# Turning activations by VectorE over all partitions and a round trip through device memory, in a two-layer macaron encoder

## The chip, the cores and the metric

The kernel runs on one core of a Trainium2 chip. Its time is device microseconds of one launch; 920.27 us is the median of three runs of the kernel before (919.97 to 920.5). One further execution was profiled; all durations below come from it.

## What is computed

Two identical layers act on a 256 x 1024 float32 array `x` (256 positions), and a last RMSNorm follows:

```python
for l in range(DEPTH):
    x = x + 0.5 * swiglu(rms_norm(x, norm_ffn1[l]), ffn1_w_gate[l], ffn1_w_up[l], ffn1_w_down[l])
    h = rms_norm(x, norm_mix[l])
    q, k, v, u, g = jnp.split(h @ w_in[l], splits, axis=-1)
    a = dilated_attention(partial_rotary(heads(q)), partial_rotary(heads(k)), heads(v))
    sg = spatial_gating(u, g, ...)
    x = x + concat([rms_norm(a), rms_norm(sg)]) @ w_out[l]
    x = x + 0.5 * swiglu(rms_norm(x, norm_ffn2[l]), ffn2_w_gate[l], ffn2_w_up[l], ffn2_w_down[l])
return rms_norm(x, final_norm)
```

`swiglu(h)` is `(silu(h @ w_gate) * (h @ w_up)) @ w_down`; the hidden width is 2816. Every weight is float32 and is used once.

## The kernel before

**Products.** The 256 positions lie in two tiles of 128 partitions (`NT`). A float32 product is made of three matmuls on float32 operands that were split into a high part and a rest: high x high, high x rest, rest x high (L165 to L167). The left operand has to be turned, so that the contracted channel lies on the partitions: `xTh`, `xTl` for `x`, and `hT` (high and rest) for the hidden activations `h`.

**Units.** The weights come as a stream of 164 units of at most four blocks of 128 x 512 (`UNITS`, 1 MB each; some hold two blocks). `load_unit` issues a unit's DMA on SP's queue into one of three `raw` buffers. `split_unit` makes the high part `whi` on ACT (L133) and the rest `wlo` on VectorE (L134), each in two instructions of 128 x 1024, into one of three buffers of each kind. `multiply` uses the unit: 4 blocks x 2 tiles x 3 = 24 matmuls on PE. A buffer comes round every third unit, so **the split of a unit has to wait until PE is done with the unit three places ahead of it in the stream**, and a load until the split of the unit three places ahead is done.

**Order.** The engines run their instructions strictly in program order. The code states an order, and the tile framework's scheduler then places each instruction by its own estimate of when it becomes ready; so an instruction can end up some places away from where the code puts it. SP's queue is in order too: a DMA that waits holds up all those behind it.

**Stages.** `ffn` works through six chunks of 512 hidden channels (the last has 256) and then through `w_down` in two passes, one for each half of `x`'s columns; `add`s bring the result into `x_sb` (L461). `mixer` starts with the first halves (channels 0 to 511) of q, k and v, and then takes their second halves. In what follows **q0, k0, v0** are the units with the first halves and **q1, k1, v1** those with the second; **a0 to a5** are the six units of the first pass through the `w_down` ahead of it, **b0 to b5** those of the second pass. a5 and b5 hold two blocks instead of four. PE takes them in the order a0 ... a5, b0 ... b5, q0, k0, v0, q1, k1, v1.

**Turning.** Where there is time, VectorE turns: its transpose swaps rows and columns within blocks of 32 x 32. `turn_blocks` (L271 to L276) uses it with 32 partitions in and another 32 partitions out, so that each block also lands in the right group of 32 partitions (a quadrant): 16 instructions of 32 x 256 for a chunk. `h_turn` and `turn_slowly` call it in four parts of four, spread between the products, and finish with the split into high part and rest (L279, L280 for `h`; L322, L323 for `x`). The first half of `x` at the start of each second ffn goes another way, through PE (`turn`). `turned` has one buffer, `h` two.

The half of `x` that is turned last is needed when PE gets to the second halves: in the mixer after three units (q0, k0, v0), at the start of an ffn after four.

Of the kernel before, what the change touches and what calls it, by code (L numbers as in the profile page):

```python
# [10 lines left out]
F32 = mybir.dt.float32  # L11
F32R = mybir.dt.float32r
BF16 = mybir.dt.bfloat16
AF = mybir.ActivationFunctionType
ALU = mybir.AluOpType
PSUM = bass.MemoryType.PSUM

P = 128
D = 1024
S = 256  # L20
NT = S // P
# [9 lines left out]
W = 512  # L31
NCH = FF // W
REM = FF - NCH * W
# [54 lines left out]
def trunk_kernel(ctx: ExitStack, tc: tile.TileContext, ws, x, cxt, rows, sgw, ident, bias, rot, out):  # L88
    nc = tc.nc
# [3 lines left out]
    big = ctx.enter_context(tc.tile_pool(name="big", bufs=1))  # L93
    act = ctx.enter_context(tc.tile_pool(name="act", bufs=4))
    small = ctx.enter_context(tc.tile_pool(name="small", bufs=4))
    ps_acc = ctx.enter_context(tc.tile_pool(name="ps_acc", bufs=4, space=PSUM))
    ps_sc = ctx.enter_context(tc.tile_pool(name="ps_sc", bufs=4, space=PSUM))

    def f32(ap):
        return ap.bitcast(F32)  # L100
# [102 lines left out]
    def accumulators(name, pool=None, tag="acc"):  # L203
        return [(pool or ps_acc).tile([P, W], F32, tag=tag, name=f"{name}{t}") for t in range(NT)]
# [8 lines left out]
    x_sb = const.tile([P, NT, D], F32, name="x_sb")  # L213
# [37 lines left out]
    def col(l, c):  # L251
        return cols_sb[:, l * NCOL + c:l * NCOL + c + 1]
# [15 lines left out]
        nc.gpsimd.tensor_tensor(v[:, 2], v[:, 1], half.to_broadcast([P, NT]), op=ALU.pow)  # L268
        return v[:, 2]

    def turn_blocks(dst, src, c):  # L271

        to = dst.rearrange("p k (t b j) -> p t k b j", t=NT, b=4)
        frm = src.rearrange("p t (k c i) -> p t k c i", c=4, i=32)
        for b in range(4):
            nc.vector.transpose(to[32 * c:32 * c + 32, :, :, b, :], frm[32 * b:32 * b + 32, :, :, c, :])  # L276

    def split_turned(dst_hi, dst_lo, src):
        nc.scalar.activation(dst_hi, src, AF.Copy)  # L279
        nc.vector.tensor_tensor(dst_lo, src, f32(dst_hi), op=ALU.subtract)  # L280
# [15 lines left out]
    class Stream:  # L296
# [16 lines left out]
        def turn_slowly(self, d, part):  # L313

            if part == 0:
                self.turned = act.tile([P, 4, S], F32, tag="turned", name="turned", bufs=1)
            turn_blocks(self.turned, x_sb[:, :, d * W:(d + 1) * W], part)
            if part == 3:
                for k in range(4):
                    g = col(self.l, self.c + 4 * d + k)  # L320
                    hi, lo = self.lhs(4 * d + k)
                    nc.scalar.activation(hi, self.turned[:, k], AF.Copy, scale=g)  # L322
                    nc.vector.scalar_tensor_tensor(lo, self.turned[:, k], g, f32(hi), op0=ALU.mult, op1=ALU.subtract)  # L323

        def given(self, k):

# [30 lines left out]
    def ffn(st, nxt, turn_second):  # L357

        hT = [[None, None] for _ in range(3)]
        turned = {}  # L360

        def h_group(f):
            a = f // 8
            if hT[a][0] is None:
                hT[a] = [big.tile([P, 8, S], F32R, tag=f"h{2 * a + n}", name=f"hT{n}") for n in range(2)]
            return hT[a]

        def h_lhs(f):
            hi, lo = h_group(f)
            return hi[:, f % 8], lo[:, f % 8]  # L370

        def h_turn(f0, h, part):

            n = h.shape[2] // P
            if part == 0:
                turned[f0] = act.tile([P, 4, S], F32, tag="turned", name="turned", bufs=1)
            turn_blocks(turned[f0][:, :n], h, part)
            if part == 3:
                for j in range(0, n, 2):
                    hi, lo = h_group(f0 + j)  # L380
                    a = (f0 + j) % 8
                    split_turned(hi[:, a:a + 2], lo[:, a:a + 2], turned[f0][:, j:j + 2])

        def gated(gate, w):
            ss = []
            for t in range(NT):
                s = act.tile([P, W], F32, tag="s", name="s")
                nc.scalar.activation(s[:, :w], gate[t], AF.Silu, scale=r[:, t:t + 1])
                ss.append(s)
            return ss  # L390

        def product(ss, up, w):
            h = act.tile([P, NT, W], F32, tag="h", name="h", bufs=2)
            for t in range(NT):
                nc.vector.scalar_tensor_tensor(h[:, t, :w], up[t], r[:, t:t + 1], ss[t][:, :w],
                                               op0=ALU.mult, op1=ALU.mult)
            return h[:, :, :w]


        accs = [accumulators("gate"), accumulators("up"),  # L400
                accumulators("gate", ps_sc, "sc"), accumulators("up", ps_sc, "sc")]
        if UNITS[done["used"]][1].endswith("_first"):
            multiply_first(accs, st.lhs)
            for i in range(len(accs)):
                turn_second(i)
        else:
            for i, acc in enumerate(accs):
                multiply(acc, st.lhs, True, False)
                turn_second(i)
        r = inverse_root(st.ssq, D)  # L410
        late = None
        for c in range(2):
            multiply(accs[2 * c], st.lhs, False, True)
            ss = gated(accs[2 * c], W)
            multiply(accs[2 * c + 1], st.lhs, False, True)
            h = product(ss, accs[2 * c + 1], W)
            if late:
                for q in range(4):
                    h_turn(*late, q)
            late = (c * W // P, h)  # L420
        for c in range(2, NCH):
            gate = accumulators("gate")
            multiply(gate, st.lhs, True, False)
            h_turn(*late, 0)
            multiply(gate, st.lhs, False, True)
            ss = gated(gate, W)
            h_turn(*late, 1)
            up = accumulators("up")
            multiply(up, st.lhs, True, False)
            h_turn(*late, 2)  # L430
            multiply(up, st.lhs, False, True)
            h_turn(*late, 3)
            late = (c * W // P, product(ss, up, W))
        both = accumulators("both")
        multiply(both, st.lhs, True, False)
        h_turn(*late, 0)
        h_turn(*late, 1)
        multiply(both, st.lhs, False, True)
        ss = gated([b[:, :REM] for b in both], REM)
        h_turn(*late, 2)  # L440
        h_turn(*late, 3)
        late = (NCH * W // P, product(ss, [b[:, REM:] for b in both], REM))
        new = None
        for d in (0, 1):
            acc = accumulators("down")
            if d == 1 and isinstance(new, Last):
                for k0 in range(0, 16, 4):
                    multiply(acc, h_lhs, k0 == 0, k0 == 12)
                new.begin(acc)
                for part in multiply_apart(h_lhs, 2):  # L450
                    new.finish(*part)
                break
            for k0 in range(0, KF, 4):
                multiply(acc, h_lhs, k0 == 0, k0 + 4 >= KF)
                if d == 0 and k0 <= 12:
                    h_turn(*late, k0 // 4)
                if d == 1 and k0 <= 12:
                    new.turn_slowly(0, k0 // 4)
            for t in range(NT):
                xs = x_sb[:, t, d * W:(d + 1) * W]  # L460
                nc.vector.scalar_tensor_tensor(xs, acc[t], 0.5, xs, op0=ALU.mult, op1=ALU.add)  # L461
            if d == 0:
                new = nxt()
            new.squares(d)
        return new
# [45 lines left out]
    def mixer(l, st, nxt):  # L511

        accs = [accumulators("q"), accumulators("k"), accumulators("v", ps_sc, "sc")]
        for i, acc in enumerate(accs):
            multiply(acc, st.lhs, True, False)
            for part in ((0, 1), (2, 3), ())[i]:
                st.turn_slowly(1, part)
        r = inverse_root(st.ssq, D)
        r8 = small.tile([P, NT], F32, tag="r8", name="r8")
# [226 lines left out]

def _stream(inputs):
    parts = []  # L750
    for l, name, ks, c in UNITS:
        if name.endswith("_first"):
            tiles = [inputs[name[:4] + m][l][c * P:(c + 1) * P, cc * W:(cc + 1) * W]
                     for cc in range(2) for m in ("_w_gate", "_w_up")]
            parts.append(np.concatenate(tiles, axis=1).reshape(-1))
            continue
        if name.endswith("_rem"):
            f = name[:4]
            w = np.concatenate([inputs[f"{f}_w_gate"][l][:, NCH * W:], inputs[f"{f}_w_up"][l][:, NCH * W:]], axis=1)
        else:  # L760
            w = inputs[name][l]
        k0, n = ks[0], len(ks)
        block = w[k0 * P:(k0 + n) * P, c * W:(c + 1) * W].reshape(n, P, W).transpose(1, 0, 2)
        parts.append(np.ascontiguousarray(block).reshape(-1))
    return np.concatenate(parts)
# [53 lines left out]
```

## Time and profile before

| | |
|---|---|
| median of three runs | 920.27 us (919.97 to 920.5) |
| the profiled execution | 922.07 us |
| its span, first to last instruction | 920.3 us |
| ScalarE (ACT) busy | 466.3 us |
| GpSimd (POOL) busy | 21.5 us |
| moved by DMA | 174.14 MB |

The span is what the profile's rows fill; 1.77 us of the profiled execution lie around it. In a group of instructions the name left of the arrow is what is written, the names right of it what is read; a line number (L276) is that of the kernel before, and lines of the changed kernel are told as such.

### The profile page before, as it was taken

To read this page: it belongs to the slowest core of one execution; us is meant where nothing else is said; L and a number is where in the kernel's file an instruction comes from. 1 tells how busy PE (TensorE), PEld (TensorE's weight loads), DVE (VectorE), ACT (ScalarE), POOL (GpSimd) and SP (SyncE) were. 2 spreads that over 40 slices of the span, in tenths; PEclk is the share of its full clock that TensorE was granted. 3 is DMA by queue.
4 is the path that set the end of the run, shared out by engine and by line. 5 is a ranking of instruction groups with operands and counts; after the bars stand their busy time and mean duration, and the time that the engine had idled before them with its cause. 6 is when DMAs were issued, how large, how long until landed. Compare 5 with 4: busy or idle time off the path is not lost.

```text
span 920.3 us, 11062 instructions
## 1 busy us (share of the span) xinstructions
PE 912.4 (99%) x4178; PEld 750.2 (82%) x4178; DVE 751.1 (82%) x1203; ACT 466.3 (51%) x654; POOL 21.5 (2%) x48
## 2 busy tenths in 40 slices
PE   9999999999999999999999999999999999999997
PEld 6888888888778888888888888888887888888886
DVE  6698996796789699896687998966887887998854
ACT  6544544356756544434445544445467545444440
POOL 0000000000010000000000000000000100000000
PEclk9999999999999999999999999999999999999999
DMA  8765555565334645646555555455543455565351
GB/s 330 297 259 183 187 201 205 187 217 192 138 113 175 215 141 206 219 147 237 192 197 177 192 213 191 152 209 208 201 140 135 164 202 183 183 210 200 126 195 47
DMA packets 26982, 174.14 MB, mean 189 GB/s; under 512 B 3120, under 2 KB 4272, under 8 KB 6960
## 3 DMA queue, kind: packets, MB, share of 16 engines
q1 hardware_dynamic: 26496, 172.86, 52.6%
q8 instruction: 33, 0.54, 0.2%
q10 hardware_dynamic: 432, 0.56, 0.2%
q14 instruction: 21, 0.17, 0.1%
HBM read 172.36 MB, written 1.05 MB: 188 GB/s over the span
## 4 chain that ended last, share of the span: by engine, by line
PE 97%; DVE 1%; issue 1%; ACT 0%; DMA 0%; POOL 0%; POOLq 0%; DVEq 0%
PE down L165 8%; PE down L166 8%; PE down L167 8%; PE gate L166 7%; PE up L166 7%; PE up L167 7%; PE gate L167 7%; PE up L165 7%; PE gate L165 7%; PE both L166 2%; PE both L165 2%; PE both L167 2%; PE g L165 1%; PE q L167 1%; PE g L166 1%; PE os L165 1%
## 5 line engine op out<-in xcount | busy, mean ns | idle before, releaser
L134 DVE TENSOR_TENSOR wlo<-raw,whi 128x1024 fp32r<-128x1024 f32 (+2 forms) x325 | 378.4, 1201 | 105.1 <-ACT whi L133 102.8
L133 ACT ACTIVATE whi<-raw 128x1024 fp32r<-128x1024 f32 (+2 forms) x325 | 322.4, 1039 | 246.9 <-issue 100.1
L276 DVE STREAM_TRANSPOSE turned<-h 32x256 f32<-32x256 f32 (+1 forms) x384 | 158.9, 414 | 6.3
L167 PE MATMUL down<-whi,hT 128*128 128x512 f32 x340 | 132.3, 389 | 0.0
L165 PE MATMUL down<-whi,hT 128*128 128x512 f32 x340 | 132.3, 389 | 0.0
L166 PE MATMUL down<-wlo,hT 128*128 128x512 f32 x340 | 132.3, 389 | 0.0
L167 PE MATMUL gate<-whi,xTl 128*128 128x512 f32 x304 | 118.3, 389 | 0.0
L167 PE MATMUL up<-whi,xTl 128*128 128x512 f32 x304 | 118.3, 389 | 0.0
L166 PE MATMUL gate<-wlo,xTh 128*128 128x512 f32 x304 | 118.3, 389 | 0.0
L165 PE MATMUL up<-whi,xTh 128*128 128x512 f32 x304 | 118.3, 389 | 0.0
L166 PE MATMUL up<-wlo,xTh 128*128 128x512 f32 x304 | 118.3, 389 | 0.0
L165 PE MATMUL gate<-whi,xTh 128*128 128x512 f32 x304 | 118.1, 389 | 0.0
L167 PEld LDWEIGHTS down<-whi,hT 128*128 128x128 f32 x340 | 63.8, 188 | 13.3
L165 PEld LDWEIGHTS down<-whi,hT 128*128 128x128 f32 x340 | 63.8, 188 | 13.3
L166 PEld LDWEIGHTS down<-wlo,hT 128*128 128x128 f32 x340 | 63.8, 188 | 13.2
L279 ACT ACTIVATE hT<-turned 128x512 fp32r<-128x512 f32 x44 | 26.8, 626 | 80.2 <-DVE turned L276 80.2
L165 PEld LDWEIGHTS gate<-whi,xTh 128*128 128x128 f32 x304 | 57.1, 188 | 11.9
L165 PEld LDWEIGHTS up<-whi,xTh 128*128 128x128 f32 x304 | 57.1, 188 | 11.9
L166 PEld LDWEIGHTS up<-wlo,xTh 128*128 128x128 f32 x304 | 57.1, 188 | 11.9
L166 PEld LDWEIGHTS gate<-wlo,xTh 128*128 128x128 f32 x304 | 57.1, 188 | 11.9
L167 PEld LDWEIGHTS up<-whi,xTl 128*128 128x128 f32 x304 | 57.1, 188 | 11.8
L167 PEld LDWEIGHTS gate<-whi,xTl 128*128 128x128 f32 x304 | 57.0, 188 | 11.8
(172 smaller groups left out, 1064.7 us busy)
## 6 DMA issues: line engine op xcount, KB each, us to landing
raw<-in_ws SPq DMA_DIRECT2D x154, 1024.0 KB, 4.8
raw<-in_ws SPq DMA_DIRECT2D x8, 512.0 KB, 3.2
raw<-in_ws SPq DMA_DIRECT2D x7, 256.0 KB, 5.5
x_sb<-in_x SPq DMA_DIRECT2D x1, 1024.0 KB, 10.8
ln_sb<-in_rows SPq DMA_DIRECT2D x1, 1024.0 KB, 7.4
out<-y SPq DMA_DIRECT2D x2, 320.0 KB, 2.5
xt_sb<-in_cxt SPq DMA_DIRECT2D x1, 512.0 KB, 7.9
sgw_sb<-in_sgw SPq DMA_DIRECT2D x1, 512.0 KB, 6.5
```

The lines of the kernel that those rows point to most:

```text
L133: nc.scalar.activation(hi[:, s], raw[:, s], AF.Copy)
L134: nc.vector.tensor_tensor(lo[:, s], raw[:, s], f32(hi[:, s]), op=ALU.subtract)
L165: nc.tensor.matmul(acc[t], xh[:, s], wh, start=start and j == 0, stop=False)
L166: nc.tensor.matmul(acc[t], xh[:, s], wl, start=False, stop=False)
L167: nc.tensor.matmul(acc[t], xl[:, s], wh, start=False, stop=stop and j == len(ks) - 1)
L276: nc.vector.transpose(to[32 * c:32 * c + 32, :, :, b, :], frm[32 * b:32 * b + 32, :, :, c, :])
L279: nc.scalar.activation(dst_hi, src, AF.Copy)
```

## The change

A turn is made in two steps. VectorE transposes the 32 x 32 blocks in place in their quadrant, over all 128 partitions at once: one instruction of 128 x 512 for each of the two tiles. Then `move_quadrants` stores the result in device memory (`far`) and loads it back with four DMAs, one for each quadrant of the destination, in rows of 512 bytes. So a turn has 2 transposes instead of 16, and 5 DMAs on SP's queue. Of the four parts of a turn only the first (transposes and moves) and the last (the split) are left. The hidden channels come out in another order within a chunk, and the rows of `w_down` are put into that order ahead of the launch (`F_ORDER`). The splits read `turned` in runs of 32 elements.

```diff
+    far = ctx.enter_context(tc.tile_pool(name="far", bufs=3, space=bass.MemoryType.DRAM))
...
-    def turn_blocks(dst, src, c):
-
-        to = dst.rearrange("p k (t b j) -> p t k b j", t=NT, b=4)
-        frm = src.rearrange("p t (k c i) -> p t k c i", c=4, i=32)
-        for b in range(4):
-            nc.vector.transpose(to[32 * c:32 * c + 32, :, :, b, :], frm[32 * b:32 * b + 32, :, :, c, :])
+    def move_quadrants(dst, tmp):
+
+        n = dst.shape[2]
+        store = far.tile([NT * P, 4 * n], F32, tag="far", name="far")
+        nc.sync.dma_start(store.rearrange("(t p) f -> p t f", p=P), tmp)
+        for c in range(4):
+            nc.sync.dma_start(dst[32 * c:32 * c + 32],
+                              store[:, c * n:(c + 1) * n].rearrange("(q i) f -> i q f", i=32))
...
         def turn_slowly(self, d, part):
             if part == 0:
-                self.turned = act.tile([P, 4, S], F32, tag="turned", name="turned", bufs=1)
-            turn_blocks(self.turned, x_sb[:, :, d * W:(d + 1) * W], part)
+                tmp = act.tile([P, NT, W], F32, tag="h", name="xB", bufs=2)
+                for t in range(NT):
+                    nc.vector.transpose(tmp[:, t].rearrange("p (c k j) -> p k c j", c=4, j=32),
+                                        x_sb[:, t, d * W:(d + 1) * W].rearrange("p (k c i) -> p k c i", c=4, i=32))
+                self.turned = act.tile([P, 4 * NT, W // 4], F32, tag="turned", name="turned", bufs=1)
+                move_quadrants(self.turned, tmp)
...
             if part == 0:
-                turned[f0] = act.tile([P, 4, S], F32, tag="turned", name="turned", bufs=1)
-            turn_blocks(turned[f0][:, :n], h, part)
+                for t in range(NT):
+                    nc.vector.transpose(h[:, t], h[:, t])
+                turned[f0] = act.tile([P, 4 * NT, W // 4], F32, tag="turned", name="turned", bufs=1)[:, :, :32 * n]
+                move_quadrants(turned[f0], h)
...
         for i, acc in enumerate(accs):
             multiply(acc, st.lhs, True, False)
-            for part in ((0, 1), (2, 3), ())[i]:
+            for part in ((0,), (), (3,))[i]:
                 st.turn_slowly(1, part)
```

The last lines are those of the mixer: the first part stands behind q0 as before, the split, which stood behind k0, now stands behind v0.

**Place 1: the start of the first mixer.** ACT's program there, in the kernel before; `whi` rows are splits (two instructions to a unit), `junk` the square sums, `xTh` the split of the turned second half of `x`, `qk<-q` the first use of what q1 finishes:

```order
L257 ACTIVATE junk,ssq<-x_sb 128x512 x2
L133 ACTIVATE whi<-raw 128x1024 x4
L322 ACTIVATE xTh<-turned,cols_sb 128x256 x4
L133 ACTIVATE whi<-raw 128x1024 x2
L526 ACTIVATE qk<-q_1482,r_1613 128x512
```

The same place of ACT's program in the changed kernel:

```order
L258 ACTIVATE junk,ssq<-x_sb 128x512
L134 ACTIVATE whi<-raw 128x1024 x2
L258 ACTIVATE junk,ssq<-x_sb 128x512
L134 ACTIVATE whi<-raw 128x1024 x6
L337 ACTIVATE xTh<-turned,cols_sb 128x256 x4
L540 ACTIVATE qk<-q_1429,r_1553 128x512
```

The last unit split ahead of `qk` is v1 in both. Before, `xTh` stands between the splits of k1 and v1; now the splits of q1, k1 and v1 all stand ahead of it.

VectorE's program at the same place, before (`x_sb<-down` are the additions at the end of the second pass, `xTl` the rest of the split of `x`, `ab` belongs to what follows q1):

```order
L461 SCALAR_TENSOR_TENSOR x_sb<-down_1271,x_sb 128x512
L461 SCALAR_TENSOR_TENSOR x_sb<-down_1272,x_sb 128x512
L134 TENSOR_TENSOR wlo<-raw,whi 128x1024 x2
L276 STREAM_TRANSPOSE turned<-x_sb 32x2x4x32 x8
L134 TENSOR_TENSOR wlo<-raw,whi 128x1024 x2
L276 STREAM_TRANSPOSE turned<-x_sb 32x2x4x32 x8
L134 TENSOR_TENSOR wlo<-raw,whi 128x1024 x2
L323 SCALAR_TENSOR_TENSOR xTl<-turned,cols_sb,xTh 128x256 x4
L134 TENSOR_TENSOR wlo<-raw,whi 128x1024 x2
L533 TENSOR_TENSOR ab<-qk,rot_sb 128x128
```

And in the changed kernel:

```order
L475 SCALAR_TENSOR_TENSOR x_sb<-down_1225,x_sb 128x512
L135 TENSOR_TENSOR wlo<-raw,whi 128x1024 x2
L475 SCALAR_TENSOR_TENSOR x_sb<-down_1226,x_sb 128x512
L135 TENSOR_TENSOR wlo<-raw,whi 128x1024 x2
L328 STREAM_TRANSPOSE xB<-x_sb 128x4x4x32 x2
L135 TENSOR_TENSOR wlo<-raw,whi 128x1024 x6
L338 SCALAR_TENSOR_TENSOR xTl<-turned,cols_sb,xTh 128x256 x4
L547 TENSOR_TENSOR ab<-qk,rot_sb 128x128
```

The same swap: `wlo` of v1 stood behind `xTl` and now stands ahead of it. k0's `wlo` has moved from ahead of the additions to between them. The second layer's mixer has v1 ahead of `xTh` and `xTl` in the same way.

SP's queue of the changed kernel at this place:

```order
L120 DMA raw<-in_ws 128x2048 x5
L276 DMA far<-xB 128x2x512
L120 DMA raw<-in_ws 128x2048
L278 DMA turned<-far 32x8x128 x4
```

The store, a load of one unit of weights, and then the four loads that bring the data back. Before, only the `raw` rows stood here.

**Place 2: the end of the first pass through the first `w_down`.** VectorE's program before, from the splits up to the first transposes:

```order
L461 SCALAR_TENSOR_TENSOR x_sb<-down_1063,x_sb 128x512
L461 SCALAR_TENSOR_TENSOR x_sb<-down_1064,x_sb 128x512
L134 TENSOR_TENSOR wlo<-raw,whi 128x1024 x2
L276 STREAM_TRANSPOSE turned<-x_sb 32x2x4x32 x7
L134 TENSOR_TENSOR wlo<-raw,whi 128x1024 x2
```

And in the changed kernel:

```order
L290 TENSOR_TENSOR hT_1017<-turned,hT_1016 128x512
L475 SCALAR_TENSOR_TENSOR x_sb<-down_1025,x_sb 128x512
L475 SCALAR_TENSOR_TENSOR x_sb<-down_1026,x_sb 128x512
L328 STREAM_TRANSPOSE xB<-x_sb 128x4x4x32
L135 TENSOR_TENSOR wlo<-raw,whi 128x1024 x2
L328 STREAM_TRANSPOSE xB<-x_sb 128x4x4x32
```

Here the `wlo` behind the additions was that of b2; it is now that of b1, with a transpose ahead of it. On PE the matmuls of a5 (12 of them, into the accumulators of the first pass, `down0_1025` and `down1_1026`) have moved behind the first 16 of b0's 24. The changed kernel's rows where they begin, with the tiles' numbers (`whi_1166` is b0's, `whi_1134` a5's):

```order
L168 MATMUL down0_1225<-whi_1166,hT1_507 128x512
L166 MATMUL down1_1226<-whi_1166,hT0_506 128x512
L166 MATMUL down0_1025<-whi_1134,hT0_1016 128x512
L167 MATMUL down0_1025<-wlo_1135,hT0_1016 128x512
L166 MATMUL down1_1026<-whi_1134,hT0_1016 128x512
L168 MATMUL down0_1025<-whi_1134,hT1_1017 128x512
```

Apart from this place and the order of two matmuls in b1, PE's program is the same as before. In the other three ffns a5 stays ahead of b0.

**Place 3: the start of an ffn.** ACT's program at the start of the first layer's second ffn, before and then in the changed kernel:

```order
L133 ACTIVATE whi<-raw 128x1024 x5
L322 ACTIVATE xTh<-turned,cols_sb 128x256 x4
L133 ACTIVATE whi<-raw 128x1024 x4
L388 ACT_TABLE_LOAD
L388 ACTIVATE s<-gate_2327,root 128x512
```

```order
L134 ACTIVATE whi<-raw 128x1024 x7
L337 ACTIVATE xTh<-turned,cols_sb 128x256 x4
L134 ACTIVATE whi<-raw 128x1024 x2
L405 ACT_TABLE_LOAD
L405 ACTIVATE s<-gate_2267,root 128x512
```

`xTh` has moved behind one more split. Here four units precede the first use of the second half, and the last split ahead of `xTh` is that of the sixth unit, which takes the buffer of the third.

More of the change, by code (lines that the diff above doesn't have):

```diff
@@ L269, in inverse_root, with turned_tile, as_blocks @@
         return v[:, 2]
-    def turn_blocks(dst, src, c):
-        to = dst.rearrange("p k (t b j) -> p t k b j", t=NT, b=4)
-        frm = src.rearrange("p t (k c i) -> p t k c i", c=4, i=32)
-        for b in range(4):
-            nc.vector.transpose(to[32 * c:32 * c + 32, :, :, b, :], frm[32 * b:32 * b + 32, :, :, c, :])
+    def move_quadrants(dst, tmp):
[5 more added lines that the diff above has]
+                              store[:, c * n:(c + 1) * n].rearrange("(q i) f -> i q f", i=32))
+    def turned_tile(turned, k, n):
+        return turned.rearrange("p q (k j) -> p k q j", j=32)[:, k:k + n]
+    def as_blocks(ap):
+        return ap.rearrange("p k (q j) -> p k q j", j=32)
     def split_turned(dst_hi, dst_lo, src):
@@ L320, in turn_slowly @@
                     g = col(self.l, self.c + 4 * d + k)
-                    hi, lo = self.lhs(4 * d + k)
-                    nc.scalar.activation(hi, self.turned[:, k], AF.Copy, scale=g)
-                    nc.vector.scalar_tensor_tensor(lo, self.turned[:, k], g, f32(hi), op0=ALU.mult, op1=ALU.subtract)
+                    hi, lo = (v[:, 4 * d + k].rearrange("p (q j) -> p q j", j=32) for v in (self.hi, self.lo))
+                    src = turned_tile(self.turned, k, 1)[:, 0]
+                    nc.scalar.activation(hi, src, AF.Copy, scale=g)
+                    nc.vector.scalar_tensor_tensor(lo, src, g, f32(hi), op0=ALU.mult, op1=ALU.subtract)
         def given(self, k):
@@ L381, in h_turn @@
                     a = (f0 + j) % 8
-                    split_turned(hi[:, a:a + 2], lo[:, a:a + 2], turned[f0][:, j:j + 2])
+                    split_turned(as_blocks(hi[:, a:a + 2]), as_blocks(lo[:, a:a + 2]), turned_tile(turned[f0], j, 2))
         def gated(gate, w):
@@ L415, in ffn @@
             multiply(accs[2 * c + 1], st.lhs, False, True)
+            if late:
+                h_turn(*late, 0)
             h = product(ss, accs[2 * c + 1], W)
[L417 to L420, printed above, removed]
+            first, late = late, (c * W // P, h)
         for c in range(2, NCH):
@@ L423, in ffn @@
             multiply(gate, st.lhs, True, False)
+            if c == 2:
+                h_turn(*first, 3)
             h_turn(*late, 0)
@@ L426, in ffn @@
             ss = gated(gate, W)
-            h_turn(*late, 1)
             up = accumulators("up")
             multiply(up, st.lhs, True, False)
-            h_turn(*late, 2)
             multiply(up, st.lhs, False, True)
@@ L436, in ffn @@
         h_turn(*late, 0)
-        h_turn(*late, 1)
         multiply(both, st.lhs, False, True)
         ss = gated([b[:, :REM] for b in both], REM)
-        h_turn(*late, 2)
         h_turn(*late, 3)
@@ L745, in trunk_kernel, with _tile_order @@
         st = ffn(st, Last if l == DEPTH - 1 else (lambda: Stream(l + 1, 0)), turn)
+def _tile_order(n, tiles):
+    return np.arange(n).reshape(-1, 4, tiles, 32).transpose(0, 2, 1, 3).reshape(-1)
+F_ORDER = np.concatenate([_tile_order(NCH * W, W // P), NCH * W + _tile_order(REM, REM // P)])
 def _stream(inputs):
@@ L761, in _stream @@
             w = inputs[name][l]
+            if name.endswith("_down"):
+                w = w[F_ORDER]
         k0, n = ks[0], len(ks)
```

## The prediction

> **What bounds the kernel now.** First the page: busy time by engine, the granted clock, and the chain of work that ended last.
>
> ```profile
> span 920.3 us, 11062 instructions
> PE 912.4 (99%) x4178; PEld 750.2 (82%) x4178; DVE 751.1 (82%) x1203; ACT 466.3 (51%) x654; POOL 21.5 (2%) x48
> PEclk9999999999999999999999999999999999999999
> PE 97%; DVE 1%; issue 1%; ACT 0%; DMA 0%; POOL 0%; POOLq 0%; DVEq 0%
> ```
>
> TensorE (PE) is busy in 912.4 of 920.3 us at full clock, and 97% of the chain is its matmuls. So time is lost or won only where PE waits. The table of waits tells where PE, or its weight load (PEld), waited once it was running:
>
> ```profile
> PEld q L167 <- DVE xTl L323: 0.5, 2, 0.2
> PE mixed L690 <- DVE vv L658: 0.2, 1, 0.2
> ```
>
> That is next to nothing: the most that a faster VectorE could give back is these 0.7 us. But the first row shows where there is no cover: at q's second half (q1) PE waits for the turned `x`, twice, once a layer. Now the timeline of that place in the first layer, first ACT, then VectorE (DVE), then PE (start, duration, what, how many):
>
> ```profile
> 187.32 2.01 ACT L133 ACTIVATE whi<-raw 128x1024 fp32r<-128x1024 f32 x2 [0.71 <-PE down L167]
> 192.81 2.01 ACT L133 ACTIVATE whi<-raw 128x1024 fp32r<-128x1024 f32 x2 [2.26 <-issue]
> 198.25 2.01 ACT L133 ACTIVATE whi<-raw 128x1024 fp32r<-128x1024 f32 x2 [3.43 <-issue]
> 201.06 1.71 ACT L322 ACTIVATE xTh<-turned,cols_sb 128x256 fp32r<-128x256 f32 x4 [0.80 <-DVE turned L276]
> 203.69 2.01 ACT L133 ACTIVATE whi<-raw 128x1024 fp32r<-128x1024 f32 x2 [0.92 <-ACT xTh L322]
> ...
> 187.97 1.28 DVE L461 SCALAR_TENSOR_TENSOR x_sb<-down,x_sb 128x512 f32<-128x512 f32 x2
> 197.43 3.60 DVE L276 STREAM_TRANSPOSE turned<-x_sb 32x256 f32<-32x256 f32 x8
> 201.06 2.36 DVE L134 TENSOR_TENSOR wlo<-raw,whi 128x1024 fp32r<-128x1024 f32 x2
> 203.34 1.67 DVE L323 SCALAR_TENSOR_TENSOR xTl<-turned,cols_sb,xTh 128x256 fp32r<-128x256 f32 x4
> 204.92 2.36 DVE L134 TENSOR_TENSOR wlo<-raw,whi 128x1024 fp32r<-128x1024 f32 x2
> ...
> 187.12 0.39 PE L165 MATMUL q<-whi,xTh 128*128 128x512 f32 x1
> 203.22 0.39 PE L167 MATMUL v<-whi,xTl 128*128 128x512 f32 x1
> 203.44 0.39 PE L165 MATMUL q<-whi,xTh 128*128 128x512 f32 x1
> 203.67 0.39 PE L166 MATMUL q<-wlo,xTh 128*128 128x512 f32 x1
> 203.90 0.47 PE L167 MATMUL q<-whi,xTl 128*128 128x512 f32 x1
> 204.21 0.39 PE L165 MATMUL q<-whi,xTh 128*128 128x512 f32 x1
> ```
>
> The splits (`whi`) of v0, q1, k1 and v1 start at 187.32, 192.81, 198.25 and 203.69. The last three steps are 5.49, 5.44 and 5.44 us: one unit of PE, 24 matmuls of about 0.227 us. v1's split starts 0.25 us after q1's first matmul (203.44), that is, when v0's last one is through. **A split is let go by PE's end of the unit three places ahead**, since it takes that unit's buffer. And `xTh` (201.06) stood ahead of v1's split, so it didn't have to wait for that.
>
> **The change, step by step.** *What goes and comes on VectorE* is read from the groups of instructions, shapes apart:
>
> ```profile
> L276 DVE STREAM_TRANSPOSE turned<-h 32x256 f32<-32x256 f32 x320 | 139.6, 436 | 5.2
> L276 DVE STREAM_TRANSPOSE turned<-x_sb 32x256 f32<-32x256 f32 x128 | 55.8, 436 | 1.8
> L276 DVE STREAM_TRANSPOSE turned<-h 32x128 f32<-32x128 f32 x64 | 19.4, 303 | 1.1
> ```
>
> 214.8 us of transposes go. 320, 128 and 64 at 16 each are 20 full turns of `h`, 8 of `x` and 4 half-wide ones of `h`. From 128 to 256 elements a transpose grows by 133 ns; two such steps more make an estimate of 436 + 2 x 133 = 702 ns for 512 elements. So 56 x 0.70 + 8 x 0.436 = 43 us come, and VectorE is freed of 172 us. Priced on the path: nothing, or at most the 0.7 us above. The splits out of `turned` keep their sizes; I take their durations as unchanged, since runs of 32 are still whole blocks, and other work lies around them everywhere but at place 1.
>
> *The DMAs* are 32 x 5 = 160 more on SP's queue, with 15 MB stored and 15 MB loaded.
>
> ```profile
> q1 hardware_dynamic: 26496, 172.86, 52.6%
> raw<-in_ws SPq DMA_DIRECT2D x154, 1024.0 KB, 4.8
> raw<-in_ws SPq DMA_DIRECT2D x8, 512.0 KB, 3.2
> xt_sb<-in_cxt SPq DMA_DIRECT2D x1, 512.0 KB, 7.9
> SPq L119 <- DVE wlo L134: 788.5, 159, 13.5
> ```
>
> 172.86 MB take 52.6% of the 16 DMA engines, so 30 MB more make some 62%. SP waits 788.5 us for buffers: a load is issued as soon as a buffer is free, takes 4.8 us, and is needed three units (16.3 us) later. That leaves 16.3 - 4.8 - 2.4 (the split) = 9 us in which SP may be held up by a store or a turned load. A turn's store and loads of 512 KB go at the 3.2 us of the 512 KB row each; the other bound is the 7.9 us that one took among the loads of the start. The turned rows of `h` stand three to five units ahead of their use, and at place 3 `xTh` waits for the end of the third unit, one unit (5.44 us) ahead of need, while whi, wlo and the first `xTl` take about 4.1. So all these are hidden and cost nothing.
>
> *Place 1, the price.* In the changed program `xTh` stands behind v1's split on ACT, and `xTl` behind v1's `wlo` on VectorE. But v1's split can't start until PE is through with v0, and the next thing PE wants is q1, which needs `xTh` and `xTl`. What hid v1's split (PE's work on q1) now waits for it. In the times of before:
>
> - ACT: v1's `whi` from 203.69, 2.01 us, to 205.70; the first `xTh` (a quarter of 1.71, about 0.5 with its tail) is there at 206.2. q1's first matmul slips from 203.44 to 206.2: 2.8 us.
> - DVE: v1's `wlo` from 204.92, 2.36 us, to 207.28; `xTl` can start at about 207.22 instead of 203.34. q1's third matmul, which needs it, came 0.56 us after `xTl` began (203.90), so it comes at 207.78: **3.9 us later**. Behind it the next quarter comes each 0.42 us and PE takes 6 matmuls (1.36 us) for each: no further wait.
>
> Is the data there by then? From PE's end of b5 (187.12) VectorE has two additions (1.28), two splits (2 x 2.36) and two transposes (1.40): 194.5. A store of 3.2 makes 197.7, a load of weights queued between 4.8, the turned loads 3.2: 205.7, just when ACT becomes free. I therefore charge nothing more. The second layer stands alike (view of ACT's timeline there):
>
> ```profile
> 654.12 1.71 ACT L322 ACTIVATE xTh<-turned,cols_sb 128x256 fp32r<-128x256 f32 x4 [0.80 <-DVE turned L276]
> 656.75 2.01 ACT L133 ACTIVATE whi<-raw 128x1024 fp32r<-128x1024 f32 x2 [0.92 <-ACT xTh L322]
> ```
>
> The distance from `xTh` to v1's split is the same 2.63 us, so 3.9 us again: **7.8 us for both**.
>
> *Place 2, the price.* b1's `wlo` now stands behind the additions of the first pass, and those wait for a5, which PE now does after 16 of b0's matmuls. From the end of a5, E, PE has the last 8 of b0 (1.81 us) and two of b1 before it wants b1's `wlo`: E + 2.27. VectorE sees E some 0.25 us later, adds (0.68), transposes (0.70) and makes the first `wlo` (1.2): E + 2.83. **0.6 us**, once. At worst the transpose takes four old ones (1.74) and it is 1.6; at best the wait is hidden.
>
> **Sum.** 7.8 + 0.6 = 8.4 us. On the profiled execution's own 922.07 us (span 920.3 and 1.77 around it) that is 930.5. The median of the three runs, 920.27, is 1.8 us lower, so for the median I forecast **928.7 us**, 0.9% slower. About 0.2% (1.8 us) is what a measurement of this kernel can tell from no change.
>
> **Rivals.** *The data comes late.* The moves of place 1 share the DMA engines with two loads of weights, and in rows of 512 bytes they may be slower. With 7.9 us for the store and for the loads the chain ends at 194.5 + 7.9 + 4.8 + 7.9 = 215.1, 9.4 us after ACT is free: 2 x 9.4 more, 947. Nearer to the 3.2 row, 2 to 4 us late at each place give 933 to 937. Against it speaks that 512 KB stand nearest to the 3.2 us of a steady stage. Chance 17%.
>
> *The clock falls.* PE stands idle for some 2.8 us and, after two matmuls, about 1.1 more. At the start of this trace PE runs slowly:
>
> ```profile
> 9.01 0.63 PE L182 MATMUL up<-whi,xTl 128*128 128x512 f32 x1
> 9.44 0.57 PE L180 MATMUL up<-whi,xTh 128*128 128x512 f32 x1
> 9.84 0.39 PE L181 MATMUL up<-wlo,xTh 128*128 128x512 f32 x1
> 10.07 0.39 PE L182 MATMUL up<-whi,xTl 128*128 128x512 f32 x1
> ```
>
> Until 9.44 matmuls follow each other at 0.43 us, from 9.84 on at 0.23. If each gap puts PE back for some 10 to 20 matmuls, that is 0.2 us each, 2 to 4 us a place: 932.7 to 936.7. Nothing in this trace shows a gap in mid-run, so it is open; chance 10%. The Trainium skill (TensorE: Matmul & The Clock Gate, section "What's actually happening") says that the clock is halved after at least one idle window of about 3.4 us and comes back after a busy window as long. By that rule a gap of 2.8 us leaves the clock alone; the start of this trace agrees as to the two speeds, and no run here shows a gap.
>
> *The wait is hidden* and the change does in place 1 what it did before: only if v1's split doesn't wait for v0. Then 920.3 to 921, within 0.2%. Against it are the three starts 5.44 us apart. Chance 6%.
>
> *Faster.* If VectorE's transposes slow PE's matmuls by sharing the memory they read, fewer of them would pay at every unit: from 0.011 us a unit on (164 units, 1.8 us), and 918 us with 0.014. Rows of a stretch with no transposes between them:
>
> ```profile
> 298.81 2.36 DVE L134 TENSOR_TENSOR wlo<-raw,whi 128x1024 fp32r<-128x1024 f32 x2 [0.40 <-ACT whi L133]
> 304.25 2.36 DVE L134 TENSOR_TENSOR wlo<-raw,whi 128x1024 fp32r<-128x1024 f32 x2 [3.08 <-ACT whi L133]
> ```
>
> 5.44 us for a unit, as with transposes under way at 197.43. Chance 2%, and it would have to outweigh place 1.
>
> **How the numbers follow.** The forecast (both waits, data in time) has 65%, late data 17%, the clock 10%, hidden 6%, faster 2%. The forecast's own range is 927 (no wait at place 2, a little less at place 1) to 931. Up to 936 it takes in most of the late data and of the clock; what lies above and the hidden and the faster cases are left out. Slower 92%, same 6%, faster 2%.
>
> **What would show it.** After: DVE busy near 580 us; waits of PE or PEld for `xTh` and `xTl` at q of some 3.5 to 4 us each, twice, and one of 0.6 us for `wlo` at the second down pass; `xTh` directly behind v1's `whi`. If ACT sits idle for a DMA ahead of `xTh`, the data was late; if matmuls after the gap are 0.43 us apart, the clock fell. No wait at q at all, or waits of PE for `raw` in the ffns, would prove me wrong.

## The result and the profile after

The changed kernel takes **935.46 us** (median of 4 runs, 934.26 to 936.72) against 920.29 us (919.97 to 920.5) for the kernel before: 1.0165 times as long, 95% interval 1.0148 to 1.0183. That is 15.2 us more, where 8.4 were forecast; it lies inside the stated range, near its upper end.

The page of the changed kernel, the lines that answer to those of before:

```profile
span 933.8 us, 10963 instructions
PE 915.4 (98%) x4178; PEld 752.0 (81%) x4178; DVE 576.2 (62%) x755; ACT 468.0 (50%) x654; POOL 21.8 (2%) x48
PEclk9999999999999999999999999999899999999999
q1 hardware_dynamic: 70016, 204.33, 66.8%
PE 91%; DMA 4%; DVE 2%; issue 1%; ACT 1%; SPq 0%; POOL 0%; POOLq 0%; ACTq 0%
```

VectorE's busy time fell from 751.1 to 576.2 us, and the span grew by 13.5. DMA is now 4% of the chain that ended last (0% before), and one of the 40 slices shows a TensorE clock below full speed, which none did before. The waits of PE, and of SP's waits the new one for the store of `x`, over the whole span (total, times, longest):

```profile
PE q L166 <- ACT xTh L337: 10.3, 2, 5.6
PE sink L361 <- DVE warm L358: 1.2, 1, 1.2
PE down L167 <- DVE wlo L135: 0.2, 1, 0.2
...
SPq L278 <- DMA far<-xB: 15.0, 6, 3.6
```

Nearly all of PE's new waiting is at q1 in the two mixers; the 0.2 us for `wlo` are place 2, and the 1.2 us at `sink` are in the kernel before too. Timeline of ACT there, first and second layer (start, duration, what, how many, idle time before it and what ended it):

```profile
197.58 2.01 ACT L134 ACTIVATE whi<-raw 128x1024 fp32r<-128x1024 f32 x2 [3.43 <-PE k L168]
202.97 2.00 ACT L134 ACTIVATE whi<-raw 128x1024 fp32r<-128x1024 f32 x2 [3.38 <-PE v L168]
208.02 1.71 ACT L337 ACTIVATE xTh<-turned,cols_sb 128x256 fp32r<-128x256 f32 x4 [3.04 <-DMA turned<-far]
215.14 1.31 ACT L540 ACTIVATE qk<-q,r 128x512 f32<-128x512 f32 x2 [5.41 <-PE q L168]
...
657.89 2.01 ACT L134 ACTIVATE whi<-raw 128x1024 fp32r<-128x1024 f32 x2 [3.43 <-issue]
663.28 2.01 ACT L134 ACTIVATE whi<-raw 128x1024 fp32r<-128x1024 f32 x2 [3.38 <-PE v L168]
667.33 1.71 ACT L337 ACTIVATE xTh<-turned,cols_sb 128x256 fp32r<-128x256 f32 x4 [2.04 <-DMA turned<-far]
675.15 1.31 ACT L540 ACTIVATE qk<-q,r 128x512 f32<-128x512 f32 x2 [6.11 <-PE q L168]
```

`xTh` stands behind v1's split (202.97), as forecast. But ACT is through with that split at 204.98 and then idles 3.04 us **for the turned loads**: the data is later than the order. Now SP's timeline and PE's around it, and the granted clock in stretches of 4 us (after the stretch: its length, busy times of PE, PEld, DVE, ACT, POOL, then the clock, DMA share and GB/s):

```profile
191.83 0.33 SPq L120 DMA_DIRECT2D raw<-in_ws  x1
193.04 0.38 SPq L276 DMA_DIRECT2D far<-xB  x1
195.63 0.33 SPq L120 DMA_DIRECT2D raw<-in_ws  x1
199.16 1.96 SPq L278 DMA_DIRECT2D turned<-far  x4
```

```profile
208.58 0.80 PE L166 MATMUL q<-whi,xTh 128*128 128x512 f32 x1 [5.65 <-ACT xTh L337]
209.18 0.63 PE L167 MATMUL q<-wlo,xTh 128*128 128x512 f32 x1
209.60 0.63 PE L168 MATMUL q<-whi,xTl 128*128 128x512 f32 x1
210.03 0.63 PE L166 MATMUL q<-whi,xTh 128*128 128x512 f32 x1
...
211.93 0.39 PE L168 MATMUL q<-whi,xTl 128*128 128x512 f32 x1
```

```profile
200.00:204.00 4.00, 2.94 (x13) 2.08 (x12) 1.04 (x1) 1.03 (x2) 0.00 (x0) 1.00 1.01 209
204.00:208.00 4.00, 0.00 (x0) 0.00 (x0) 2.36 (x2) 0.98 (x2) 0.00 (x0) 1.00 0.93 238
208.00:212.00 4.00, 3.42 (x9) 2.75 (x10) 1.69 (x4) 1.71 (x4) 0.00 (x0) 0.57 0.66 264
212.00:216.00 4.00, 4.00 (x19) 3.31 (x18) 0.14 (x1) 0.86 (x2) 0.00 (x0) 1.00 0.00 0
```

PE stands for 5.65 us. When it goes on, its matmuls follow each other at 0.43 us instead of 0.23. The mean clock of that stretch of 4 us is 0.57, so 4 x (1 - 0.57) = 1.7 us of full speed are missing, about 1.6 of them behind the gap. So each place costs a gap and then a slow start.

**The account.** The same instructions in the kernel before (ACT's timeline; the first row of the four, 198.25, stands in the prediction):

```profile
208.57 1.31 ACT L526 ACTIVATE qk<-q,r 128x512 f32<-128x512 f32 x2 [2.87 <-PE q L167]
...
651.31 2.01 ACT L133 ACTIVATE whi<-raw 128x1024 fp32r<-128x1024 f32 x2 [3.43 <-issue]
...
661.62 1.31 ACT L526 ACTIVATE qk<-q,r 128x512 f32<-128x512 f32 x2 [2.85 <-PE q L167]
```

| instruction | before | after | later by | gained since the row above |
|---|---|---|---|---|
| k1's split, layer 1 | 198.25 | 197.58 | -0.67 | -0.67 |
| first use of q, layer 1 | 208.57 | 215.14 | 6.57 | **7.24** |
| k1's split, layer 2 | 651.31 | 657.89 | 6.58 | 0.01 |
| first use of q, layer 2 | 661.62 | 675.15 | 13.53 | **6.95** |
| end of the span | 920.3 | 933.8 | 13.5 | -0.03 |

Nothing is lost or won between the two mixer starts, nor behind the second. The -0.67 is made of a start that was quicker by chance and of 1.0 us lost since, 0.3 among the first units and 0.7 at place 2. In the profiled execution of before the matmuls were 0.43 us apart until 9.84 us, in this one until about 7 us, and the first of them began 0.46 us sooner here: 1.65 us together (the same matmul starts at 9.84 and at 8.19). The medians don't hold that accident, so they lie 15.2 us apart and the spans 13.5.

### The profile page after: what moved, and what is told of

Its sections match the earlier page's. It is cut to its first block, busy times and chain, and to the rows that moved or that the text cites. A ratio compares the mean times of both kernels' runs of the same rounds, so it can differ in the third digit from the quotient of the medians.

```text
span 933.8 us, 10963 instructions
## 1 busy us (share of the span) xinstructions
PE 915.4 (98%) x4178; PEld 752.0 (81%) x4178; DVE 576.2 (62%) x755; ACT 468.0 (50%) x654; POOL 21.8 (2%) x48
## 3 DMA queue, kind: packets, MB, share of 16 engines
q1 hardware_dynamic: 70016, 204.33, 66.8%
## 4 chain that ended last, share of the span: by engine, by line
PE 91%; DMA 4%; DVE 2%; issue 1%; ACT 1%; SPq 0%; POOL 0%; POOLq 0%; ACTq 0%
PE down L167 8%; PE down L168 8%; PE down L166 8%; PE gate L168 7%; PE up L168 7%; PE gate L166 7%; PE up L166 7%; PE up L167 7%; PE gate L167 7%; DMA turned<-far 2%; PE both L168 2%; PE both L167 2%; PE both L166 2%; DMA far<-xB 1%; DMA raw<-in_ws 1%
## 5 line engine op out<-in xcount | busy, mean ns | idle before, releaser
L405 ACT ACTIVATE s<-gate,root 128x512 f32<-128x512 f32 x40 | 27.2, 690 | 53.8 <-PE gate L168 53.8
L412 DVE SCALAR_TENSOR_TENSOR h<-up,root,s 128x512 f32<-128x512 f32 x40 | 28.5, 750 | 18.2 <-PE up L168 18.1
```

## The experiments

Each kernel was timed beside the kernel before on the same chip (its median there 920.4 to 920.5 us). Where an instruction is "held" behind another, the scheduler was told to leave the marked instructions in the order of the code (`keep_in_program_order`). Diffs are cut to what matters; `...` stands for lines left out.

**Order alone (e1).** Kernel before; part 4 is the split of `x` only, held behind v1's split:

```diff
...
             for part in ((0, 1), (2, 3), ())[i]:
-                st.turn_slowly(1, part)
+                st.turn_slowly(1, part, 4)
+        run_ahead(done["used"] + 1)
+        st.turn_slowly(1, 4, 4)
```

> The kernel before with one thing changed: in both mixers the split of x's turned second half (xTh, xTl) stands behind v1's split on ScalarE and VectorE. No new DMA. If order is what costs (the forecast): PE idle about 2.8 us ahead of q1's first matmul and about 1.1 us more behind its second, twice; 7.8 us more than before, 928.1 us, and full clock behind the gap. If a gap of 2.8 us already lowers the clock: 1.5 to 2 us more at each place, 931 to 932 us. If order is worth nothing by itself: 920.3 us.

Measured: 928.21 us, ratio 1.0080 (1.0065 to 1.0096). The 7.8 us are there, but they are made up of other terms than I had, so that the time fits is in part luck. PE's waits, and its clock in the first layer:

```profile
PE q L165 <- ACT xTh L324: 5.0, 2, 2.5
```

```profile
204.00:206.00 2.00, 0.79 (x2) 0.70 (x3) 2.00 (x2) 2.00 (x5) 0.00 (x0) 0.79 0.80 324
206.00:208.00 2.00, 2.00 (x6) 1.51 (x6) 1.79 (x5) 0.36 (x1) 0.00 (x0) 0.50 0.82 205
208.00:210.00 2.00, 2.00 (x9) 1.65 (x8) 0.00 (x0) 0.00 (x0) 0.00 (x0) 0.86 0.95 397
```

A gap of 2.5 us, twice, with no wait for `xTl` behind it: in this program PE has matmuls on `xTh` of q1 and k1 to do meanwhile. But the clock falls already after 2.5 us: 2 x (0.21 + 0.50 + 0.14) = 1.7 us lost at the first place. The four executions took 927.56, 927.59, 928.83 and 929.79 us, the last being the profiled one, with a mean granted clock of 0.997 in the two faster ones and 0.995 in the two slower. An estimate: a fall at one place (1.7 us, or 0.002 of the mean) would explain that difference, so the clock may have fallen at one place only in the faster ones; they have no trace.

**The order put back in the changed kernel (e2).** v1's split (units 39 and 121) is held behind `xTh`:

```diff
+            pin = tc.keep_in_program_order if i in (39, 121) else (lambda ins: ins)
-            nc.scalar.activation(hi[:, s], raw[:, s], AF.Copy)
-            nc.vector.tensor_tensor(lo[:, s], raw[:, s], f32(hi[:, s]), op=ALU.subtract)
+            pin(nc.scalar.activation(hi[:, s], raw[:, s], AF.Copy))
+            pin(nc.vector.tensor_tensor(lo[:, s], raw[:, s], f32(hi[:, s]), op=ALU.subtract))
```

> The changed kernel, with v1's split held behind the split of x's turned half in both mixers, as in the kernel before. If order is what costs: the wait at q1 goes, about 7.8 us less than the changed kernel, 927.7 us. If the data is late: ScalarE waits for the turned loads in any case, the first xTh starts at about 208.0 us as in the changed kernel, PE waits the same 5.6 us and the clock falls the same; 935.5 us within 1 us.

Measured: 934.69 us, 1.0156 (1.0142 to 1.0170): no difference from the changed kernel that can be told. ACT now waits at the head of its queue:

```profile
206.73 1.71 ACT L338 ACTIVATE xTh<-turned,cols_sb 128x256 fp32r<-128x256 f32 x4 [7.15 <-DMA turned<-far]
```

7.15 us for the turned loads. They land a little sooner here (6.0 us instead of 7.2), so `xTh` starts at 206.73 and PE waits 4.4 us, where 208.0 and 5.6 were expected. So order costs 7.8 us by itself, and undoing it wins next to nothing: the late data stands behind it.

**The old turn in the mixers only (e3).** The changed kernel with 16 transposes of 32x256 and no DMA for `x`'s second half in the mixers:

```diff
...
-            for part in ((0,), (), (3,))[i]:
-                st.turn_slowly(1, part)
+            for part in ((0, 1), (2, 3), ())[i]:
+                st.turn_old(1, part)
```

> The changed kernel, with x's second half in both mixers turned the old way (16 transposes of 32x256, no DMA); the 30 other turns stay new. If the whole cost sits at the two mixer starts: 920.3 us and the 0.8 us of the first ffn's down passes, 921.1 us. If the other 30 turns or the larger DMA volume cost something in many small pieces: more than 922 us.

Measured: 920.72 us, 1.0005 (0.9996 to 1.0014); the same as before. Two of 32 turns cost 14.7 of the 15.2 us; the other 30, with VectorE at 587.1 us, bring nothing and cost at most 1.3 us (the interval's upper end).

**The gap filled (e4).** The changed kernel with spare matmuls between v0 and q1; their results aren't used:

```diff
+        sink = ps_sc.tile([P, W], F32, tag="sc", name="sink")
+        idle = st.hi[:, 0:2].rearrange("p k s -> p (k s)")
+        for i in range(24):
+            tc.keep_in_program_order(nc.tensor.matmul(sink, st.hi[:, 0, :P], idle, start=True, stop=True))
```

> The changed kernel, with 24 spare matmuls of 128x512 (results unused) on PE between v0 and q1 in both mixers: 24 x 0.227 = 5.4 us, about as long as the gap. If the slow matmuls behind the gap come from PE's idleness (the clock): they go, and 1.4 + 2.1 = 3.5 us with them; 932.0 us, though the gap itself stays filled with useless work. If they come from anything else (the operands just written, the DMAs): 935.5 us.

Measured: 932.26 us, 1.0127 (1.0113 to 1.0141). More work on the engine that bounds, and 3.2 us less than the changed kernel. PE's timeline and the clock at the first place:

```profile
202.66 5.61 PE L535 MATMUL sink<-xTh 128*128 128x512 f32 x24
208.10 0.40 PE L166 MATMUL q<-whi,xTh 128*128 128x512 f32 x1
208.33 0.40 PE L167 MATMUL q<-wlo,xTh 128*128 128x512 f32 x1
```

```profile
206.00:210.00 4.00, 4.00 (x19) 3.22 (x19) 2.00 (x5) 1.71 (x4) 0.00 (x0) 1.00 0.75 246
```

q1 begins at about the same time and at full speed. The slow matmuls come from PE's idleness.

**One hop instead of two (e5, e6).** In the mixers the transposed half goes straight from on-chip memory to on-chip memory; in e5 `xTh` stays behind v1's split, in e6 v1's split is held behind it besides:

```diff
...
-                move_quadrants(self.turned, tmp)
+                    to = self.turned.rearrange("p (t b) f -> p t b f", b=4)
+                    for c in range(4):
+                        for b in range(4):
+                            nc.sync.dma_start(to[32 * c:32 * c + 32, :, b, :],
+                                              tmp[32 * b:32 * b + 32, :, c * P:(c + 1) * P])
...
```

> The changed kernel, but in both mixers the transposed half of x goes between quadrants in one hop (16 DMAs from on-chip memory to on-chip memory, 32 partitions each) instead of a store and four loads; xTh still stands behind v1's split. If two transfers in a row make the data late: it lands before ScalarE is through with v1's split (205.0 us), ScalarE no longer waits for a DMA, PE's gap shrinks from 5.6 to the 2.5 us of the order-only kernel, and with some 2 us of half clock at each place the time is 929 to 930.5 us. If any move through the DMA queue is late here: ScalarE still waits for a DMA and the time stays at 935 us.

> One hop as before and, besides, v1's split held behind xTh. If lateness and order together are the whole cost (each alone leaves the other standing): both gaps go, 920.7 to 921.5 us, as with the old turn in the mixers. If the one hop is later than 203 us: a gap of that size remains.

Measured: e5 930.49 us (1.0092 to 1.0122), a time as expected, though in the first layer ACT still waited 0.75 us for the data and PE's gap was 3.4 us (2.5 in the second). e6 929.63 us (1.0082 to 1.0112), where 921 was expected if the data came in time. It didn't; the tile `turned` in e6, first layer:

```profile
L336 SPq DMA_DIRECT2D turned<-xB x16: 594/596/1492, 192.4 to 203.1; - x16
DMA to landing us min/median/max: 1.8/1.9/4.1
```

The median one lands in 1.9 us, but SP issues one per 0.6 us, so the sixteenth leaves only at 203.1. I had hoped for data in time, and that failed; but e6 told something else. PE's waits in its two mixers, the first and the second:

```profile
PE q L167 <- ACT xTh L345: 3.7, 1, 3.7
...
PE q L167 <- ACT xTh L345: 1.9, 1, 1.9
```

Behind the 3.7 us the clock fell (0.50 in the stretch from 208 to 210 us), behind the 1.9 us, which ended at 662.9, it didn't:

```profile
664.00:666.00 2.00, 2.00 (x10) 1.64 (x9) 1.54 (x3) 1.96 (x3) 0.00 (x0) 1.00 1.00 422
```

**The load of weights behind the turned loads (e7).** Same bytes, another place in SP's queue (units 40 and 122):

```diff
-            nc.sync.dma_start(t[:, c:c + step], src[:, c:c + step])
+            ins = nc.sync.dma_start(t[:, c:c + step], src[:, c:c + step])
+            if i in (40, 122):
+                tc.keep_in_program_order(ins)
```

> The changed kernel; in both mixers the one load of weights that stands in SP's queue between the store of x and its four turned loads is put behind those loads. Same bytes, same order on the other engines. If the store (6.0 us) and the loads (7.3 us) are slow because that load shares the DMA engines: the store lands in about 4.5 us, the turned loads about 2 to 3 us earlier, PE's gap is 2.6 to 3.6 us, and the time 930 to 931.5 us. If they are slow by themselves (short rows): no change, 935.5 us.

Measured: 931.19 us, 1.0114 (1.0099 to 1.0129). The time of the turned loads from issue to landing, in the changed kernel and then in e7:

```profile
DMA to landing us min/median/max: 6.8/7.2/7.3
```

```profile
DMA to landing us min/median/max: 2.4/2.8/3.0
```

**The rows of 512 bytes aren't slow by themselves; the 1 MB load ahead of them in the queue held them up.** In the changed kernel that load, issued at 195.63, lands only at 205.06, and the first of the four turned loads 0.9 us later. The store stayed at 5.8 us (6.0 in the changed kernel; 4.5 was expected), so it wasn't that load which stretched it. Another load, issued at 191.83, stands just ahead of the store. Where that one went behind the turned loads too (e10, below), the store still took 4.6 us in the first mixer and 5.5 in the second, so what stretches the store stays open. With the data in time, what is left in e7 is the gap of order (2.5 us at each place), in one mixer 0.7 us for `xTl`, and the clock.

**Fewer spare matmuls (e8).** 18 instead of 24.

> The changed kernel with 18 spare matmuls (4.1 us) in the gap instead of 24, so that PE idles for about 1.6 us at each place. The order-only kernel showed half clock behind an idle time of 2.5 us, the time of 932.3 us with 24 shows none behind 0.2. If 1.6 us are enough to lower the clock: 3 to 3.5 us more than with 24, about 935.5 us. If not: 932.3 us, as with 24.

Measured: 930.67 us (1.0091 to 1.0125). It doesn't answer its question: PE idled 0 and 0.8 us, not 1.6. In the first mixer the turned loads landed sooner (3.8 us instead of 7.2), although the 1 MB load stood ahead of them as before: the store took 7.3 us, so they left 1.0 us later, and that load landed at 202.95 instead of 205.06. In the second mixer they took 7.5 to 7.9 us. So e8 shows no fall of the clock behind 0.8 us, and that the lateness itself varies.

**Both chains put right (e9, e10).** e9 is e2 and e7 together. e10 also has the two transposes ahead of the next split on VectorE, and one more load of weights behind the turned ones:

```diff
...
+        st.turn_slowly(1, 0)
         for i, acc in enumerate(accs):
             multiply(acc, st.lhs, True, False)
-            for part in ((0,), (), (3,))[i]:
+            for part in ((), (), (3,))[i]:
```

> The changed kernel with two things of the order put right in both mixers: v1's split held behind xTh, and the load of weights behind the four turned loads. Each alone left a gap of 2.5 us or more. If the cost is the later of two chains (order, data): the data lands near 202.5 us, xTh starts at once, PE's gap is below 1 us, too short for the clock, and the time is 921.5 to 923 us. If something else delays q1: 928 us or more remain.

> As the one before, and the two transposes of x stand behind the additions at once, ahead of the next split on VectorE (2.3 us earlier), so that the store leaves 2 us earlier; the next load of weights also goes behind the turned loads. If the sum of the chain (transposes, store, loads) is all that is left: the data lands at about 200 us, no gap at all, 920.7 to 921.2 us, no faster than the kernel before, since PE had no wait there. If freeing VectorE of 170 us is worth anything: below 919.5 us.

Measured: e9 922.7 us, 1.0031 (1.0016 to 1.0045); the data landed at 203.3 us, 0.8 later than expected, and PE waited 1.5 us at q1 in the first mixer and not at all in the second. e10 920.84 us, 1.0003 (0.9994 to 1.0011), the same as before. ACT in e9 and in e10:

```profile
203.49 1.71 ACT L340 ACTIVATE xTh<-turned,cols_sb 128x256 fp32r<-128x256 f32 x4 [4.29 <-DMA turned<-far]
```

```profile
199.87 1.71 ACT L340 ACTIVATE xTh<-turned,cols_sb 128x256 fp32r<-128x256 f32 x4 [0.67 <-DMA turned<-far]
```

e2 alone won 0.8 us and e7 alone 4.3; together they win 12.8. In e10 the data is there at 199.8 us, and PE has no wait at q1 in either mixer. It has the new turn everywhere, VectorE at 575.8 us, and no gain: the freed time was on no path. No version here beats the kernel before, and with PE busy 911 to 912 of 919 to 920 us in before, e3 and e10 there is little to beat.

**The clock without DMAs (e11).** e1 with 4 spare matmuls in the gap:

> The order-only kernel (the kernel before, xTh behind v1's split) with 4 spare matmuls (0.9 us) in the gap, which shortens PE's idle time from 2.5 to 1.6 us; no DMA is involved, so the gap doesn't vary. If 1.6 us are too short to lower the clock: no slow matmuls, 1.7 us less at each place, 924.5 to 926 us, although PE does more. If the clock falls all the same: 928 us.

Measured: 925.9 us, 1.0055 (1.0040 to 1.0070). PE's waits, and its clock behind the first:

```profile
PE q L165 <- ACT xTh L324: 3.2, 2, 1.6
```

```profile
204.00:206.00 2.00, 1.51 (x7) 1.25 (x8) 2.00 (x4) 1.64 (x5) 0.00 (x0) 1.00 0.99 418
206.00:208.00 2.00, 2.00 (x10) 1.67 (x9) 1.07 (x3) 0.00 (x0) 0.00 (x0) 1.00 0.70 201
```

q1 can't start sooner than in e1, yet the kernel is 2.3 us faster, since after 1.6 us the clock stayed full in both layers.

## Why the prediction was right, and where it was not

The sign, the place and the bound were right. Of the 15.2 us, 8.4 were forecast, and the time lies above the 927 to 931 of the forecast's own case. By its steps:

- **What bounds, and what VectorE's freed time is worth: right.** Forecast nothing; e3 and e10 are within 0.05% of before. The estimate of 702 ns for a transpose of 128x512 met 692 to 699, VectorE's 580 us met 576.2.
- **The other 30 turns are hidden: right.** The account has 0.01 us between the mixers and -0.03 behind them, although the DMA engines were busier than reckoned (66.8% instead of some 62).
- **Place 2, 0.6 us: right within what can be told.** In the changed kernel the weight load waited 0.7 us for b1's `wlo` and the matmuls behind came some 0.7 us late; e3, which keeps place 2, is 0.3 us over before with an interval of about 0.9 to each side.
- **Place 1, the price of order, 3.9 us each: the sum was right, one term not.** e1 measured 7.8 for both. The gap was 2.5 us (forecast 2.8), but the 1.1 us for `xTl` did not come there, and the clock took its place with some 1.7. That the two nearly cancel is luck.
- **"I therefore charge nothing more" for the data: wrong.** This is the step that failed. I had the chain end at 205.7; it ended at 207.9, in an execution that ran 0.67 us ahead at this place. VectorE was through sooner than I reckoned (193.0 instead of 194.5), but the store took 6.0 us and the turned loads 7.2, not 3.2 each, and the four took 2 us to issue. I took the time of 512 KB from a steady stage in which one load at a time runs; here the store had the load of 191.83 beside it and the turned loads that of 195.63 ahead of them, and the DMA share was 1.01 from 200 to 204 us and 0.93 in the next 4. I had put the load of 195.63 into the chain at 4.8 us; it took 9.4, and the turned loads landed behind it. By e7 its place in the queue cost 4.3 us for both mixers. The 3.2 us were too small all over the changed kernel (median 6.5 us for the stores of `h`, 5.3 for the turned loads); elsewhere the slack hid that.
- **The clock, kept as a rival: it fell at both places**, for 1.7 and 2.3 us. I held a gap of 2.8 us for probably too short. The Trainium skill (TensorE: Matmul & The Clock Gate, section "What's actually happening") has the clock halved after at least one idle window of about 3.4 us. By that rule e1's gaps of 2.5 us would have left it alone; its trace differs, and the measurement decides: a stretch of that length shows in the traces, but it need not be idle as a whole (last section).
- **How the cases were put together: wrong.** I gave late data 17% and the clock 10% as cases beside the forecast. They aren't alternatives to it: the gap is the later of the two chains (order 2.5, data 5.6 and 4.6 us), a gap of either cause can bring the clock down, and both happened. 5.6 + 1.7 and 4.6 + 2.3 make 7.3 and 6.9, which is the account's 7.24 and 6.95. The upper bound of the range, which came from those rivals, is what held the result: that the time lies within it owes something to luck, since I took each rival for unlikely and both came true.

## What to carry to other kernels

Where a change makes one instruction wait for two chains (an order on its engine and a transfer), price both and take the later. Undoing the earlier one alone then shows almost nothing (e2), undoing the later one wins only the difference (e7), and both have to be undone to see the cost go (e9, e10). A small transfer on a tight path wants its place in the queue ahead of the bulk loads, not merely enough bandwidth on average. And add to any gap on TensorE what it takes to come back to speed: in e1's trace each gap of 2.5 us cost 1.7 more.

## What the runs showed of the hardware

**When the clock falls.** The half clock set in behind shorter gaps than expected, and the traces show when. In each trace the changes of the clock in mid-run lie whole multiples of 3.41 us apart. In the changed kernel, for instance, the granted clock is 0.61 from 208 to 209 us and 0.80 from 665 to 666, so it fell at 208.22 and at 665.60: 457.38 us, or 134 x 3.413. In e1, e2, e5 and e7 the two falls are 457.4 us apart as well, while their gaps began 457.3 to 459.4 us apart. Half clock lasted 3.41 us or twice that; of the longer ones PE still waited through a part, so that in the changed kernel's second layer it ran for 4.5 of the 6.8 us. So each trace can be cut into windows of 3.41 us, counted from its falls (where there is none, from the moment near the start at which the clock became full, which lies on the same beat in the others). Idle time of PE at q1, the most of it that lies in one window, and the clock:

| kernel, layer | PE's waits at q1, us | most in one window, us | half clock, us |
|---|---|---|---|
| e8, second | 0.8 | 0.8 | none |
| e9, first | 1.5 | 1.5 | none |
| e11, both | 1.6 and 1.6 | 1.6 and 1.0 | none |
| e6, second | 1.9 | 1.7 | none |
| e1, both | 2.5 and 2.5 | 2.4 and 2.5 | 3.4 and 3.4 |
| e5, both | 3.4 and 2.5 | 2.4 and 2.4 | 3.4 and 3.4 |
| e7, both | 2.5 + 0.7 and 2.5 | 2.3 and 2.5 | 3.4 and 3.4 |
| e6, first | 3.7 | 2.2 | 3.4 |
| e2, both | 4.4 and 4.7 | 3.2 and 2.5 | 3.4 and 6.8 |
| changed kernel, both | 5.6 and 4.6 | 3.4 and 2.4 | 3.4 and 6.8 |

All eleven falls stand at the end of a window with 2.2 us or more of idle time. No window with 1.9 us or less ended in one: in the changed kernel's first layer the window that ended at 204.81 held 1.9 us, and the clock fell only at the end of the next. Between 1.9 and 2.2 us no run here tells. So it matters where in a window a gap begins; by this a gap of 2.5 us that a window's end cuts in halves would leave the clock alone, which no trace here shows.

**A small load behind a large one.** With the 1 MB load ahead of them on the same queue, the four loads of 128 KB took 3.4 to 7.9 us (changed kernel, e2, e4, e8). In both mixers of each the first of them landed 0.6 to 0.9 us after that load, which itself took 7.5 to 9.4 us there. With the load behind them they took 2.3 to 3.2 us (e7, e9, e10).

**Issue.** A DMA from on-chip memory to on-chip memory over 32 partitions took SP 0.6 us to issue (e6), against 0.45 us for one of the turned loads, so that 16 of them were bound by their issue.
